# A two-layer mixture-of-experts block on one core: the loop for left-over tokens ahead of the experts' last half, and a final norm of one chain per token tile

## Chip, cores and metric

The kernel runs on one core of a Trainium2 chip. The metric is the device time of one execution in microseconds (us); smaller is better. Times shown are the median of three runs, with the lowest and the highest. The profile and its trace are of one execution.

## What is computed

The reference is a block of two post-norm layers over 256 latent tokens, with 256 context tokens that pass through the same weights (model width 1024, all in fp32). In each layer three token mixers (attention, gated linear attention, neighbourhood attention) are merged and normed, then a hierarchical mixture of 32 experts follows, and a last norm:

```python
def layer_norm(x, g, b):
    return layer_norm0(x) * g + b
...
    def expert_block(inp):
        xb, e = inp
        return (jax.nn.silu(xb @ w1[e]) * (xb @ w3[e])) @ w2[e]
```

`x = LayerNorm(alpha * x + gate2 * HierMoE(h2))`: each token chooses one group of experts and the two best experts in it; the outputs come back to the token weighted by its gates. The next layer begins with `h = LN0(x) * (1 + scale1) + shift1`. Layer 0 needs both streams (512 tokens, T = 4 tiles of 128), the experts of layer 1 only the latents (T = 2).

## The kernel before

Tokens stand on the partitions, a tile of [128, 1024] each (`x1[t]`). The 32 experts of a layer are worked on in halves of 128 slots: 14 halves in layer 0 (the experts ranked by load, with one, two or four experts in a half), 16 halves of two experts in layer 1. An expert has six pieces of weights of [128, 2048], 1 MB each: four of w1 and w3, two of w2. The tile buffers `ew`, `ewb` and a few spare ones hold 9 pieces in layer 0 and 14 in layer 1. SyncE (SP) issues every load, in the order of its queue, and each issue waits until the buffer's last reader is done.

`experts` (line 1471) goes through the halves. `front` gathers the tokens of two halves to XT. `body` makes the two first products: h <- ew, XT at line 1506, four parts for a half of two experts, one for each pair of pieces. `tail` calls `expert_tail` (line 1398): silu on ScalarE, act on VectorE, a transpose (aT, lines 1406 and 1407), then the second product Y <- ew, aT at line 1414 in two parts n = 0, 1 of 512 columns, each split into Yh (line 806, ScalarE) and Yl (line 807, VectorE). `combine` brings Y back to the tokens: cb (lines 1428 and 1429), ct = cb times gate (line 1431), x += ct (line 1432). The tail of half n stands behind the body of half n + 1, so that TensorE has the body to do while the small steps run; after the last body come the tails of the last two halves.

`overflow` (line 1533) takes the tokens that found no slot. Its `For_i` loop (line 1545) runs once for every block of 128 such tokens; the count is read from memory, and it is zero here in both layers. It stands behind `experts`. `final_norm` (line 1581) norms the tiles in batches of two with `stats_all` (lines 336 to 346: bn_stats for each tile, then Newton's method on columns of both tiles). In layer 0 ScalarE's identity (line 1596), VectorE's product with g (1597) and the sum with b (1598, on GpSimdE, POOL, but for one tile) follow, and two tiles are stored for later (line 1600); in layer 1 VectorE does it alone (lines 1589 and 1592) and the output is stored (1594). `final_loads` (line 1604) loads g and b, spread over the partitions (`lgb`, 2 x 512 KB). Then layer 1 begins: `modulation` loads wmod (line 493) for the products tmod (line 495), `norm_T` (line 532) norms again with `stats_all`, makes xh (line 539) on ScalarE and transposes it (hT, line 550); the projections pT of the mixers come next.

What the engines do in which order is set by a scheduler, which places every instruction by the priority of its place in the program and by its operands; `later(n)` puts pieces back. A program loop is a place that it doesn't schedule across: what stands ahead of the loop in an engine's order stays ahead of it.

Of the kernel before, what the change touches and what calls it, by code (L numbers as in the profile page):

```python
# [21 lines left out]
NL = 2  # L22
# [36 lines left out]
# columns of the per-partition biases  # L59
# [9 lines left out]
# sections of the constants  # L69
# [9 lines left out]
# ranks of the experts of layer 0, by load but for experts 0 and 1, whose weights come in early:  # L79
# with 128 slots, with 64, the others with 32; the order of their halves of 128 slots  # L80
# [29 lines left out]
def groups(l):  # L110
    """The experts (in layer 0 by rank of their load) that share 256 slots, in two halves of one, two or four experts"""
# [10 lines left out]
def _constants():  # L122
# [20 lines left out]
    # slots of the experts by rank  # L143
# [15 lines left out]
    # pairs of tokens of a block of 64 whose highest different bit is the level's  # L159
# [5 lines left out]
def _layout(inp):  # L165
    """The arrays of setup_inputs() as the program reads them."""
# [6 lines left out]
    # w_mod: [layer, group of four 512-column chunks, k tile, half of the group][partition][2 chunks x 512]  # L173
# [10 lines left out]
    # branches in the order in which they are merged: gla, attention, neighbourhood  # L184
# [42 lines left out]
    # the relative bias of every (query, key), outside of the window a constant; context keys have none  # L227
# [12 lines left out]
    # experts: [layer, expert][partition][six pieces of 2048]  # L240
# [9 lines left out]
class _Prog:  # L250
# [3 lines left out]
    # ---- tiles  # L254
# [14 lines left out]
    def rsqrt(self, v, w, tmp=None):  # L269
        """v ** -0.5 by Newton's method"""  # L270
# [34 lines left out]
    def norm0(self, x, xh, total=None):  # L305
        """xh = layer_norm0(x), both [128, 1024]; with the sums of x, ScalarE makes those of its squares"""
# [15 lines left out]
    def stats_all(self, xs, apart=False):  # L322
        """stats of tiles together: columns of means, of 1 / sqrt(var + eps), and of the opposites of their products"""
# [25 lines left out]
    def norm_quick(self, x, out, g, b):  # L349
        """out = layer_norm0(x) * g + b, on VectorE alone, and the sums of its rows; x is overwritten"""  # L350
# [7 lines left out]
    def norm(self, x, out, g, b, last=None):  # L358
        """layer_norm0(x) * g + b, in two steps"""
# [24 lines left out]
    def projT(self, l, n, ntok):  # L384
        """[128 columns of w_in, tokens] = w^T h^T"""
# [7 lines left out]
    def projM(self, l, names, kper, width, tiles, sub=None):  # L393
        """[tokens, columns of w_in] for the token tiles, one bank each"""
# [17 lines left out]
    # ---- constants  # L412
# [42 lines left out]
    def open(self, name, side, tags):  # L455
        """A pool that shares its place with the one that follows it on the same side"""
# [7 lines left out]
    def later(self, n=400):  # L464
        """What is traced here gives way to the next n instructions"""
# [4 lines left out]
    # ---- modulation  # L470
    def modulation(self, l, groups, tag="raw", tag2="b2", ps="mod"):
        """[128, 512] of group g: row 32 j + s holds 512-column chunk 4 g + j for the latents (s = 0) and the context (s = 1)"""
# [11 lines left out]
        for g in groups:  # L484
# [19 lines left out]
            # the columns: [partition, scale or shift, stream, k tile]  # L504
# [18 lines left out]
    def mod_row(self, l, q, s, tag="o4"):  # L523
        """A modulation vector on every partition: [128, 1024]"""
# [7 lines left out]
    def norm_T(self, l, xs):  # L532
        """h^T of the mixers: modulated layer_norm0 of the four token tiles, in two parts"""
        nc = self.nc
        xh = []
        for a in range(0, 4, NT[l]):
# [1174 lines left out]
```

## Time and profile before

| | |
|---|---|
| runs, median (lowest to highest) | 2171.39 us (2170.97 to 2172.95) |
| profiled execution, span | 2169.8 us |
| TensorE (PE) busy | 1989.3 us, 92% |
| VectorE (DVE) busy | 968.1 us, 45% |
| ScalarE (ACT) busy | 561.9 us, 26% |
| GpSimdE (POOL) busy | 272.2 us, 13% |
| loaded and stored | 562.41 MB, mean 259 GB/s |

The span runs from the first to the last instruction of the profiled execution; no other time is given for it, and the median of the runs is 1.6 us above it. In the rows, "x16" counts instructions, "[1.33 <-DMA ew]" is idle time of the engine ahead of them and what ended it, a name with "q" (SPq) is an engine's sequencer, where it waits or issues. PE entries are single passes: a product of the program has two of them where its operands are fp32. A share of busy time is a mean over stages with different limits, so the stages are read one by one.

### The profile page before, as it was taken

The page shows a single profiled execution, that of the slowest core. Times are in us where ns is not written, and L with a number is a line of the kernel's source. Part 1 is how long each engine was busy: PE and PEld are TensorE (multiplying, and loading weights), DVE is VectorE, ACT ScalarE, POOL GpSimd, SP SyncE. Part 2 cuts the span into 40 slices and gives each one's busy share as a digit, 9 for nine tenths or more (in the row PEclk, how much of TensorE's full clock was granted, in tenths as well). Part 3 has the DMA queues.
Part 4 walks back from the last instruction along what each step waited for, and adds up shares of the span by engine and source line. Part 5 has one row for each costly group of instructions (what it writes and reads, how often), then busy time and mean ns, then how long its engine had stood idle before and what let it go on. Part 6 is the DMA issues. An engine that isn't in the chain of part 4 may idle for free. (4 is left out here: it accounts for less than half of the span.)

```text
span 2169.8 us, 28061 instructions
## 1 busy us (share of the span) xinstructions
PE 1989.3 (92%) x10749; PEld 1179.2 (54%) x10749; DVE 968.1 (45%) x2236; ACT 561.9 (26%) x992; POOL 272.2 (13%) x260
## 2 busy tenths in 40 slices
PE   5999999999998898989899598999996999999995
PEld 2676766777885353445253165786795433333321
DVE  4676765564388131222022765766648222221213
ACT  3443334343333000000000254444543111010000
POOL 1322100011110010111011222100020000000000
PEclk9999999999999999999999798999997999999998
DMA  7436212223328899999998723632466999999995
GB/s 289 164 121 218 78 59 69 93 83 96 126 79 334 367 420 421 371 385 421 419 369 370 270 85 112 197 118 74 139 207 250 387 421 423 421 423 422 421 422 222
DMA packets 113987, 562.41 MB, mean 259 GB/s; under 512 B 13302, under 2 KB 14838, under 8 KB 72120
## 3 DMA queue, kind: packets, MB, share of 16 engines
q1 hardware_dynamic: 113272, 558.85, 66.9%
q8 instruction: 87, 1.43, 0.3%
q10 hardware_dynamic: 576, 1.70, 0.2%
q14 instruction: 52, 0.43, 0.1%
HBM read 557.36 MB, written 3.15 MB: 258 GB/s over the span
## 5 line engine op out<-in xcount | busy, mean ns | idle before, releaser
L1506 PE MATMUL h<-ew,XT 128*64 128x512 f32 (+2 forms) x2048 | 478.3, 611 | 40.0 <-DMA ew<-in_ew_dram 39.8
L1506 PEld LDWEIGHTS h<-ew,XT 128*64 128x64 f32 (+2 forms) x2048 | 146.6, 135 | 326.3 <-issue 248.8
L1414 PE MATMUL Y<-ew,aT 128*64 128x512 f32 (+2 forms) x1024 | 252.4, 598 | 10.1 <-DMA ew<-in_ew_dram 7.9
L292 DVE TENSOR_TENSOR wlo<-raw,whi 128x1024 fp32r<-128x1024 f32 (+1 forms) x140 | 178.9, 1278 | 139.6 <-ACT whi L291 138.4
L1432 POOL TENSOR_TENSOR x<-x,ct 128x512 f32<-128x512 f32 x82 | 105.0, 1307 | 1003.5 <-DVE ct L1431 879.8
L380 PE MATMUL pT<-hThi,whi 128*128 128x512 f32 (+1 forms) x576 | 202.9, 352 | 1.5 <-ACT whi L291 0.8
L291 ACT CAST whi<-raw 128x1024 fp32r<-128x1024 f32 (+1 forms) x140 | 145.4, 1039 | 226.5 <-PE pT L381 116.2
L382 PE MATMUL pT<-hThi,wlo 128*128 128x512 f32 (+1 forms) x576 | 202.3, 351 | 0.2 <-DVE wlo L292 0.2
L381 PE MATMUL pT<-hTlo,whi 128*128 128x512 f32 (+1 forms) x576 | 202.1, 351 | 0.0
L1403 DVE SCALAR_TENSOR_TENSOR act<-h,s,sl 128x512 f32<-128x512 f32 x30 | 22.5, 751 | 325.4 <-PE h L1506 270.5
L1414 PEld LDWEIGHTS Y<-ew,aT 128*64 128x64 f32 (+2 forms) x1024 | 76.0, 133 | 151.0 <-issue 125.7
L807 DVE TENSOR_TENSOR Yl<-Y,Yh 128x512 fp32r<-128x512 f32 x60 | 41.4, 690 | 257.2 <-ACT Yh L806 254.1
L806 ACT CAST Yh<-Y 128x512 fp32r<-128x512 f32 x60 | 35.2, 587 | 462.5 <-PE Y L1414 462.5
L380 PEld LDWEIGHTS pT<-hThi,whi 128*128 128x128 f32 x576 | 109.5, 190 | 22.4 <-issue 4.1
L382 PEld LDWEIGHTS pT<-hThi,wlo 128*128 128x128 f32 x576 | 109.5, 190 | 16.2 <-issue 2.9
L381 PEld LDWEIGHTS pT<-hTlo,whi 128*128 128x128 f32 x576 | 109.6, 190 | 15.2 <-issue 3.0
L380 PE MATMUL pM<-whi,hThi 128*128 128x512 f32 (+1 forms) x304 | 110.7, 370 | 3.6 <-ACT qTkT L645 1.9
L381 PE MATMUL pM<-wlo,hThi 128*128 128x512 f32 (+1 forms) x304 | 111.8, 369 | 0.0
L382 PE MATMUL pM<-whi,hTlo 128*128 128x512 f32 (+1 forms) x304 | 111.7, 368 | 0.0
L495 PE MATMUL mod<-wmod,sT 128*32 128x512 f32 x320 | 75.0, 624 | 23.4 <-DVE s L343 14.8
L1407 ACT COPY aT<-aT 128x512 f32<-128x512 f32 x30 | 17.6, 586 | 292.7 <-PE aT L1406 292.7
L1383 PE MATMUL XT<-OH,h2hi 128*128 128x256 f32 x352 | 89.1, 290 | 0.0
(363 smaller groups left out, 3093.4 us busy)
## 6 DMA issues: line engine op xcount, KB each, us to landing
ew<-in_ew_dram SPq DMA_DIRECT2D x326, 1024.0 KB, 13.8
raw<-in_w_dram SPq DMA_DIRECT2D x145, 512.0 KB, 3.7
ew<-in_ew_dram SPq DMA_DIRECT2D x116, 512.0 KB, 13.5
wmod<-in_wmod_dram SPq DMA_DIRECT2D x96, 512.0 KB, 6.1
nb<-in_nb_dram SPq DMA_DIRECT2D x32, 256.0 KB, 3.8
g<-md SPq DMA_DIRECT2D x12, 256.0 KB, 7.6
row<-in_ln_dram SPq DMA_DIRECT2D x4, 512.0 KB, 4.9
lgb<-in_ln_dram SPq DMA_DIRECT2D x4, 512.0 KB, 12.0
```

The lines of the kernel that those rows point to most:

```text
L291: self.nc.scalar.copy(hi, src)
L292: (eng or self.nc.vector).tensor_tensor(lo, src, hi.bitcast(F32), op=ALU.subtract)
L380: mm(out, lh, rh, start=start, stop=False)
L381: mm(out, lh, rl, start=False, stop=False)
L382: mm(out, ll, rh, start=False, stop=stop)
L495: nc.tensor.matmul(p[32 * j:32 * j + 32, :], self.sT[:, k, :], raws[j // 2][:, 512 * (j % 2):512 * (j % 2) + 512], start=k == 0, stop=k == 7)
L806: self.nc.scalar.copy(hi, src)
L807: self.nc.vector.tensor_tensor(lo, src, hi.bitcast(F32), op=ALU.subtract)
L1383: mm(p[:, w * j:w * j + w], self.h2s[t][part][:, 128 * k:128 * k + 128], OH[:, t], start=t == 0 and part == 0, stop=t == T - 1 and part == 1)
L1414: mm(y[m * i:m * i + m, :], aT[:, 128 * f + m * i:128 * f + m * i + m], w2(f, n, i), start=f == 0, stop=f == 3)
L1432: (nc.vector if last and n else nc.gpsimd).tensor_tensor(self.x1[t][:, ns], self.x1[t][:, ns], tmp, op=ALU.add)
L1506: mm(h[m * i:m * i + m, :], XTs[dp][:, k, 128 * pr + m * i:128 * pr + m * i + m], w[i, 2 * q + k // 4][k % 4], start=k == 0, stop=k == 7)
```

## The change

The edits, by function:

- `experts`: when the last half comes, four of its pieces are loaded, then the tail of the half before it is made, then `overflow`, then the last body. g and b are loaded ahead of the last tail, in both layers, to a tile of "e8".
- `load`: w2 of the last half comes in pieces of 512 KB, those of the two experts in turn; `expert_tail` loses the order by expert that it had there.
- `overflow`: the loop's body takes weights in pieces of [128, 512] in "ct" buffers, and gets the slots of its tokens by transposing the one-hot matrix.
- `final_norm`: for each tile one chain on VectorE: bn_stats, mean and variance, Newton's method on [128, 1], (x - mean) g, then r and b; in layer 0 the last step also sums the rows.
- `norm_T`, layer 1: from these sums ScalarE makes the sum of squares (Square), VectorE the root, ScalarE xh, tile by tile.
- `run`: `final_norm` comes before the buffers of layer 0 are given back and those of layer 1's mixers are opened.

```diff
     def norm_T(self, l, xs):
-        for a in range(0, 4, NT[l]):
+        for t in range(4 if l else 0):
+            h, st = self.t([128, 1024], ("whi", "wlo")[t % 2], name="xh"), self.small(20)
+            nmu, v, m = (st[:, i:i + 1] for i in range(3))
+            nc.vector.tensor_scalar(nmu, self.total[t], -1.0 / 1024, None, op0=ALU.mult)
+            nc.scalar.activation(h, xs[t], AF.Square, bias=nmu, accum_out=v)
+            nc.vector.tensor_scalar(v, v, 1.0 / 1024, EPS, op0=ALU.mult, op1=ALU.add)
+            r = self.rsqrt(v, 1, st[:, 3:6])
+            nc.vector.tensor_tensor(m, nmu, r, op=ALU.mult)
+            nc.scalar.activation(h, xs[t], AF.Identity, bias=m, scale=r)
+            xh.append(h)
+        for a in range(0, 0 if l else 4, NT[l]):
...
     def load(self, l, us, n, js, step=2048, most=99, after=None):
         for j in js:
+            if step < 2048:
+                xs = [self.t([128, 2048], "ew", name="ew") for _ in us]
+                self.nw += len(us)
+                for v in range(0, 2048, step):
+                    for i, x in enumerate(xs):
+                        self.nc.sync.dma_start(x[:, v:v + step], w["src"][i][:, j, v:v + step])
...
     def experts(self, l, T):
...
         def tail(dp, pr, us, hs):
-            end = SPL and 2 * dp + pr == len(halves) - 1
-            self.load(l, us, 2 * dp + pr, (4,))
-            self.load(l, us, 2 * dp + pr, (5,), 1024 if end else 2048)
+            end = 2 * dp + pr == len(halves) - 1
+            self.load(l, us, 2 * dp + pr, (4, 5), 1024 if end else 2048)
...
-            with self.later(0 if n else FIRST):
-                held[n] = body(*x)
-            if n:
+            if n == len(halves) - 1:
+                self.load(l, x[2], n, range(4), most=4)
+                tail(*halves[n - 1], held[n - 1])
+                self.overflow(l, T)
+            held[n] = body(*x)
+            if 0 < n < len(halves) - 1:
                 tail(*halves[n - 1], held[n - 1])
+        lgb = self.final_loads(l)
         tail(*halves[-1], held[len(halves) - 1])
+        return lgb
...
     def final_norm(self, l, T, lgb):
+        self.total = []
+        for t in range(T):
+            x, st = self.x1[t], self.small(20)
+            for i in range(2):
+                nc.vector.bn_stats(st[:, 6 * i:6 * i + 6], x[:, 512 * i:512 * i + 512])
+            nc.vector.bn_aggr(st[:, 12:14], st[:, 0:12])
+            mu, v = st[:, 12:13], st[:, 14:15]
+            nc.vector.tensor_scalar(v, st[:, 13:14], EPS, None, op0=ALU.add)
+            r = self.rsqrt(v, 1, st[:, 15:18])
+            STT(x, x, mu, g, op0=ALU.subtract, op1=ALU.mult)
+            if l == NL - 1:
+                for i in range(2):
+                    s = slice(512 * i, 512 * i + 512)
+                    STT(x[:, s], x[:, s], r, b[:, s], op0=ALU.mult, op1=ALU.add)
+                    nc.sync.dma_start(self.out[0, 128 * t:128 * t + 128, s], x[:, s])
+                continue
+            self.total.append(st[:, 18:19])
+            STT(x, x, r, b, op0=ALU.mult, op1=ALU.add, accum_out=st[:, 18:19])
+            if t < 2:
+                nc.sync.dma_start(self.x2[t], x)
...
     def run(self):
-            self.experts(l, T)
-            if l:
-                lgb = self.final_loads(l)
-            self.overflow(l, T)
+            lgb = self.experts(l, T)
+            xs = self.final_norm(l, T, lgb)
             if l == 0:
...
                 left, right = self.mixers(1)
-                lgb = self.final_loads(l)
-            xs = self.final_norm(l, T, lgb)
```

How the engines' orders change is seen at three places. In the rows an instruction's line is that of its own program (before: loop 1545, h 1506, Y 1414; changed: loop 1570, h 1524, Y 1423), and "waits" names the queues and engines that it waits for (DMAHW0 to 7 are queues of loads).

**TensorE at the end of layer 1.** In the changed program (Y_15927 is Y of half 14, h_16211 and h_16228 are the body of half 15, Y_16273 and Y_16284 its Y):

```order
L1423 MATMUL Y_15927<-ew_15899,aT_15905 64x512 [waits DMAHW6_49,PE_49]
L1423 MATMUL Y_15927<-ew_15901,aT_15905 64x512 [waits DMAHW7_49]
...
L1569 TENSOR_LOAD r_4_13744 [waits DVE_49]
L1570 COMPARE_AND_BRANCH
L1570 UNCONDITIONAL_BRANCH [waits PE_49]
...
L1524 MATMUL h_16211<-ew_13766,XT_15609 64x512
L1524 MATMUL h_16211<-ew_13768,XT_15609 64x512
...
L1524 MATMUL h_16228<-ew_16203,XT_15609 64x512
L1524 MATMUL h_16228<-ew_16205,XT_15609 64x512
...
L1423 MATMUL Y_16273<-ew_16248,aT_16262 64x512 [waits Activation_49]
...
L1423 MATMUL Y_16284<-ew_16254,aT_16262 64x512 [waits DMAHW2_49,PE_49]
```

Before (h_15836 is the body of half 15, Y_15874 and Y_15885 Y of half 14, Y_15921 Y of half 15), the body stood ahead of Y of half 14, and each piece's first product had its own wait for a load:

```order
L1406 MATMUL aT_15866<-cst,act_15862 128x128 x3
L1506 MATMUL h_15836<-ew_15813,XT_15525 64x512 [waits DMAHW5_49]
...
L1506 MATMUL h_15836<-ew_15815,XT_15525 64x512 [waits DMAHW6_49]
L1506 MATMUL h_15836<-ew_15817,XT_15525 64x512 [waits DMAHW7_49]
L1506 MATMUL h_15836<-ew_15815,XT_15525 64x512
...
L1414 MATMUL Y_15874<-ew_15853,aT_15863 64x512 [waits DMAHW0_49,Activation_49]
...
L1414 MATMUL Y_15885<-ew_15857,aT_15863 64x512 [waits DMAHW2_49,PE_49]
...
L1414 MATMUL Y_15921<-ew_13680,aT_15910 64x512 [waits DMAHW5_49]
```

The body of half 15 has moved behind the loop, where its products have no wait for a load; only the Y whose weights are loaded behind the loop has one.

**SyncE at the end of layer 1.** Before (ew_15811 to 15817 are w1 and w3 of half 15, ew_15853 to 15859 w2 of half 14, the pieces behind them w2 of half 15):

```order
L1463 DMA ew_15811<-in_ew_dram 128x2048 [waits DMAHW4_49,PE_49]
L1463 DMA ew_15813<-in_ew_dram 128x2048 [waits DMAHW5_49,PE_49]
...
L1463 DMA ew_15853<-in_ew_dram 128x2048 [waits DMAHW0_49,PE_49]
L1463 DMA ew_15855<-in_ew_dram 128x2048 [waits DMAHW1_49,PE_49]
L1463 DMA ew_15857<-in_ew_dram 128x2048 [waits DMAHW2_49,PE_49]
L1463 DMA ew_15859<-in_ew_dram 128x2048 [waits DMAHW3_49,PE_49]
L1468 DMA ew_13678<-in_ew_dram 128x1024 [waits DMAHW4_49,PE_49]
L1468 DMA ew_13680<-in_ew_dram 128x1024 [waits DMAHW5_49,PE_49]
...
L1468 DMA ew_13685<-in_ew_dram 128x1024 [waits DMAHW3_49,PE_49]
L1545 COMPARE_AND_BRANCH
```

In the changed program (ew_15895 to 15901 are w2 of half 14, ew_16203 to 16209 w1 and w3 of half 15, ew_16248, 16249, 16254 and 16255 its w2):

```order
L1481 DMA ew_15895<-in_ew_dram 128x2048 [waits DMAHW4_49,PE_49]
...
L1481 DMA ew_15901<-in_ew_dram 128x2048 [waits DMAHW7_49,PE_49]
L1481 DMA ew_16203<-in_ew_dram 128x2048 [waits DMAHW0_49,PE_49]
L1481 DMA ew_16205<-in_ew_dram 128x2048 [waits DMAHW1_49,PE_49]
L1481 DMA ew_16207<-in_ew_dram 128x2048 [waits DMAHW2_49,PE_49]
L1481 DMA ew_16209<-in_ew_dram 128x2048 [waits DMAHW3_49,PE_49]
L1464 DMA ew_16248<-in_ew_dram 128x1024 [waits DMAHW6_49,DMAHW4_49,PE_49]
L1464 DMA ew_16249<-in_ew_dram 128x1024 [waits DMAHW7_49,DMAHW5_49,PE_49]
...
L1570 COMPARE_AND_BRANCH
...
L1642 DMA lgb_16245<-in_ln_dram 128x1024 x2
L1464 DMA ew_16254<-in_ew_dram 128x1024 [waits PE_49]
L1464 DMA ew_16255<-in_ew_dram 128x1024 [waits PE_49]
```

w2 of half 14 is now loaded ahead of the last pieces of half 15's body; g and b and the second pair of w2 have moved behind the loop.

**SyncE between the layers.** Before (lgb are g and b of layer 0; wmod is for tmod of layer 1):

```order
L1463 DMA ew_8669<-in_ew_dram 128x1024 [waits DMAHW6_49]
L1545 COMPARE_AND_BRANCH
...
L1611 DMA lgb_9051<-in_ln_dram 128x1024
L1611 DMA lgb_9052<-in_ln_dram 128x1024
L493 DMA wmod_9238<-in_wmod_dram 128x1024
L493 DMA wmod_9239<-in_wmod_dram 128x1024
L493 DMA wmod_9246<-in_wmod_dram 128x1024 [waits DMAHW7_49]
```

In the changed program (ew_8946 to 8952 are pieces of the last half's body, cs is a table for the rope instructions on VectorE, x the stores):

```order
L1481 DMA ew_8946<-in_ew_dram 128x2048 [waits DMAHW5_49,PE_49]
...
L1481 DMA ew_8948<-in_ew_dram 128x2048 [waits DMAHW6_49,DMAHW2_49,PE_49]
...
L1481 DMA ew_8950<-in_ew_dram 128x2048 [waits DMAHW7_49,DMAHW3_49,PE_49]
L1570 COMPARE_AND_BRANCH
...
L1642 DMA lgb_8988<-in_ln_dram 128x1024 x2
...
L1481 DMA ew_8952<-in_ew_dram 128x2048 [waits PE_49]
...
L583 DMA cs_9408<-in_cst_dram 128x256 [waits DMAHW3_49,DMAHW7_49,DMAHW1_49,PE_49]
...
L1634 DMA x_0_77<-x_1063_5260 128x1024 [waits DMAHW5_49,DVE_49,Pool_49]
L1634 DMA x_1_78<-x_1077_5379 128x1024 [waits DMAHW6_49,DVE_49,Pool_49]
L493 DMA wmod_9322<-in_wmod_dram 128x1024 [waits DMAHW0_49]
L493 DMA wmod_9323<-in_wmod_dram 128x1024
```

Loads of the last half stand on both sides of the loop, and the loads of wmod have moved behind the stores of x, which wait for VectorE.

## Rows read from the trace of the kernel before

**Rows 1.** Stretches: us, busy of PE, PEld, DVE, ACT, POOL, clock, DMA share, GB/s.
```profile
700.00:1177.00 477.00, 440.26 (x2246) 200.81 (x2246) 105.79 (x185) 38.87 (x66) 61.08 (x48) 0.97 0.96 394
...
1187.00:1207.00 20.00, 15.22 (x53) 7.05 (x51) 10.01 (x16) 1.17 (x2) 5.02 (x4) 0.96 0.02 7
...
1680.00:2144.00 464.00, 444.56 (x2045) 174.70 (x2046) 97.60 (x178) 46.32 (x80) 36.38 (x28) 1.00 1.00 414
```

**Rows 2.** Waits of SyncE (SPq), 1170 to 1240: us, times, longest.
```profile
SPq L1545 <- remote: 26.6, 1, 26.6
```

**Rows 3.** Timeline of TensorE, end of layer 0: start, us, [idle before].
```profile
1144.07 3.65 PE L1506 MATMUL h<-ew,XT 128*64 128x512 f32 x14 [1.33 <-DMA ew<-in_ew_dram]
...
1156.56 3.65 PE L1506 MATMUL h<-ew,XT 128*64 128x512 f32 x16
...
1192.40 1.20 PE L1428 MATMUL cb<-Yh,C 128*128 128x512 f32 x4
...
1194.46 3.65 PE L1414 MATMUL Y<-ew,aT 128*64 128x512 f32 x8
...
1223.93 1.05 PE L495 MATMUL tmod<-wmod,sT 128*32 128x512 f32 x4 [0.23 <-DMA wmod<-in_wmod_dram]
...
1262.39 0.39 PE L380 MATMUL pT<-hThi,whi 128*128 128x256 f32 x1
```

**Rows 4.** Timeline of VectorE around the loop of layer 0.
```profile
1204.33 1.28 DVE L1432 TENSOR_TENSOR x<-x,ct 128x512 f32<-128x512 f32 x2
...
1206.24 0.69 DVE L1432 TENSOR_TENSOR x<-x,ct 128x512 f32<-128x512 f32 x1
1208.65 4.84 DVE L336 BATCH_NORM_STATS2 s<-x 128x6 f32<-128x512 f32 x8 [1.71 <-issue]
...
1214.89 0.29 DVE L343 SCALAR_TENSOR_TENSOR s<-s 128x2 f32<-128x2 f32 x2
```

**Rows 5.** Timeline of ScalarE behind it.
```profile
1207.82 1.86 ACTq L373 DMA_DIRECT2D raw<-in_w_dram  x3
...
1237.65 4.63 ACT L539 ACTIVATE xh<-x,s 128x1024 f32<-128x1024 f32 x4 [16.13 <-DVE s L346]
```

**Rows 6.** Groups between the layers, 1207 to 1262: count, busy us, mean ns, idle before.
```profile
L495 PE MATMUL tmod<-wmod,sT 128*32 128x512 f32 x64 | 20.0, 724 | 18.8 <-DMA wmod<-in_wmod_dram 18.8
...
L1597 DVE TENSOR_TENSOR x<-x,lgb 128x1024 f32<-128x1024 f32 x4 | 8.9, 2298 | 1.2 <-ACT x L1596 1.2
```

**Rows 7.** Timeline of TensorE, end of layer 1.
```profile
2114.26 3.65 PE L1506 MATMUL h<-ew,XT 128*64 128x512 f32 x16 [1.43 <-DMA ew<-in_ew_dram]
...
2119.25 3.65 PE L1506 MATMUL h<-ew,XT 128*64 128x512 f32 x16 [0.75 <-DMA ew<-in_ew_dram]
2124.20 3.22 PE L1506 MATMUL h<-ew,XT 128*64 128x512 f32 x13 [1.30 <-DMA ew<-in_ew_dram]
...
2146.68 3.66 PE L1414 MATMUL Y<-ew,aT 128*64 128x512 f32 x12
```

**Rows 8.** Stretches as in rows 1, around TensorE's pauses.
```profile
1206.00:1222.00 16.00, 4.32 (x10) 0.56 (x12) 12.89 (x43) 4.64 (x4) 2.55 (x1) 0.50 0.83 318
1222.00:1224.00 2.00, 1.77 (x10) 0.21 (x8) 2.00 (x2) 0.00 (x0) 2.00 (x2) 0.86 1.02 408
...
1234.00:1242.00 8.00, 3.04 (x12) 1.62 (x12) 5.25 (x43) 4.35 (x4) 0.00 (x0) 0.50 1.03 405
1242.00:1244.00 2.00, 2.00 (x12) 0.80 (x10) 0.91 (x3) 1.11 (x4) 0.00 (x0) 0.74 0.90 260
```

**Rows 9.** DMA issues of the page: count, KB, us from issue to landing.
```profile
raw<-in_w_dram SPq DMA_DIRECT2D x145, 512.0 KB, 3.7
```

**Rows 10.** Timeline of VectorE, end of layer 1.
```profile
2159.18 1.27 DVE L1589 SCALAR_TENSOR_TENSOR x<-x,s,lgb 128x1024 f32<-128x1024 f32 x1
...
2161.82 0.16 DVE L343 SCALAR_TENSOR_TENSOR s<-s 128x2 f32<-128x2 f32 x1
2162.02 0.16 DVE L344 TENSOR_TENSOR s<-s 128x2 f32<-128x2 f32 x1
```

More of the change, by code (lines that the diff above doesn't have):

```diff
@@ L1396, in spots, with expert_tail @@
         return C
-    def expert_tail(self, h1, h3, gate, w2, halves, end=False):
+    def expert_tail(self, h1, h3, gate, w2, halves):
         nc, mm = self.nc, self.nc.tensor.matmul
@@ L1411, in expert_tail @@
             m = 128 // halves
-            order = [(f, i) for f in range(4) for i in range(halves)]
-            for f, i in sorted(order, key=lambda x: x[1]) if end else order:
+            for f, i in [(f, i) for f in range(4) for i in range(halves)]:
                 mm(y[m * i:m * i + m, :], aT[:, 128 * f + m * i:128 * f + m * i + m], w2(f, n, i), start=f == 0, stop=f == 3)
@@ L1448, in load @@
         for j in js:
+            if step < 2048:
[4 more added lines that the diff above has]
+                        self.nc.sync.dma_start(x[:, v:v + step], w["src"][i][:, j, v:v + step])
+                for i, x in enumerate(xs):
+                    w[i, j] = [x[:, 512 * v:512 * v + 512] for v in range(4)]
+                continue
             for i in range(len(us)):
@@ L1461, in load @@
                         self.nc.gpsimd.tensor_copy(x[0:32, 0:1], after[0:32, 0:1])
-                    for v in range(0, 2048, step):
-                        self.nc.sync.dma_start(x[:, v:v + step], src[:, v:v + step])
+                    self.nc.sync.dma_start(x, src)
                     w[i, j] = [x[:, 512 * v:512 * v + 512] for v in range(4)]
@@ L1568, in overflow @@
                 for k in range(8):
-                    mm(h, XT[:, k], w[2 * m + k // 4][:, 512 * (k % 4):512 * (k % 4) + 512], start=k == 0, stop=k == 7)
+                    mm(h, XT[:, k], piece(8 * m + k), start=k == 0, stop=k == 7)
                 hs.append(h)
-            Y = self.expert_tail(hs[0], hs[1], gate, lambda f, n, i: w[4 + n][:, 512 * f:512 * f + 512], 1)
-            col = self.small(1)
-            nc.vector.tensor_tensor(col, sel, c["pcol"][:, 0:1], op=ALU.add)
-            self.combine([(self.spots(self.slot_rows(self.over, T), col, T),) + Y], T, False)
+            Y = self.expert_tail(hs[0], hs[1], gate, lambda f, n, i: piece(16 + 4 * n + f), 1)
+            p = self.ps("row")
+            for t in range(T):
+                nc.tensor.transpose(p[:, 128 * t:128 * t + 128], OH[:, t].bitcast(F32), self.ident)
+            C = self.t([128, 128 * T], "o1", F32R, "C")
+            nc.vector.tensor_copy(C, p[:, :128 * T])
+            self.combine([(C,) + Y], T, False)
             nc.vector.tensor_scalar(cnt, cnt, 1.0, None, op0=ALU.add)
@@ L1582, in final_norm @@
         nc = self.nc
-        x = self.x1
+        STT = nc.vector.scalar_tensor_tensor
         g, b = lgb
-        for a in range(0, T, NB[l]):
-            ts = range(a, a + NB[l])
-            for t, (mu, r, m) in zip(ts, self.stats_all([x[t] for t in ts], APF[l])):
-                if t in FQ[l]:
-                    nc.vector.scalar_tensor_tensor(x[t], x[t], mu, g, op0=ALU.subtract, op1=ALU.mult)
-                    for i in range(2):
-                        s = slice(512 * i, 512 * i + 512)
-                        nc.vector.scalar_tensor_tensor(x[t][:, s], x[t][:, s], r, b[:, s], op0=ALU.mult, op1=ALU.add)
-                        if l == NL - 1:
-                            nc.sync.dma_start(self.out[0, 128 * t:128 * t + 128, s], x[t][:, s])
-                else:
-                    nc.scalar.activation(x[t], x[t], AF.Identity, bias=m, scale=r)
-                    nc.vector.tensor_tensor(x[t], x[t], g, op=ALU.mult)
-                    (nc.vector if t in FD else nc.gpsimd).tensor_tensor(x[t], x[t], b, op=ALU.add)
-                if t < 2 and l < NL - 1:
-                    nc.sync.dma_start(self.x2[t], x[t])
@@ L1603, in final_loads @@
+        return self.x1
     def final_loads(self, l):
         nc = self.nc
-        if l:
-            x = self.t([128, 2, 1024], "e8", name="lgb")
-            lgb = [x[:, 0], x[:, 1]]
-        else:
-            lgb = [self.t([128, 1024], "g4", name="lgb") for _ in range(2)]
+        x = self.t([128, 2, 1024], "e8", name="lgb")
+        lgb = [x[:, 0], x[:, 1]]
         for i in range(2):
```

21 lines of the change are left out of this document (10 added, 11 removed).

## The prediction

> **What bounds the kernel now.** I read the busy time by stage first. In both expert stages the weights set the pace: the DMA engines are busy 0.96 of the time from 700 to 1177 us (layer 0) and 1.00 from 1680 to 2144 (layer 1); from 1187 to 1207 they stand at 0.02 [rows 1]. SyncE's waits say why: the engine that issues the loads sits 26.6 us at line 1545, the loop [rows 2]. The loop makes no trip (no instruction of its body is in the trace), but all engines meet there. Next the timelines. In layer 0 TensorE's last Y runs from 1194.46 to 1198.1 [rows 3]; VectorE adds until 1206.93, meets the others, and goes on 1.71 us later [rows 4]; from there a chain of two norms leads to the last xh of ScalarE, 1237.65 + 4.63 = 1242.28 [rows 5], on which layer 1's transposes hang. In layer 1 TensorE waits for each pair of 1 MB pieces: 2114.26, 2119.25, 2124.20 [rows 7], 4.98 us a pair, 2.49 a MB. The last Y ends at 2150.3, the span 19.5 us later.
>
> **The loop, layer 0.** The change puts the loop behind Y of half 12 and ahead of the last body, with weights in flight. In the order of the changed program the products behind the loop have no wait for the weights loaded ahead of it; those for weights loaded behind it do. So the loop itself must wait until every transfer in flight has landed. Everything here rests on this step.
> When does it release? At 1144.07 a piece has just landed [rows 3]. In the new order the tenth after it is the last that Y(12) needs: 1144.07 + 10 x 2.49 = 1169.0, and Y's second part takes 3.65: 1172.6. Only then is a slot free for the last MB ahead of the loop, ew_8950, which travels alone. 512 KB take 3.7 us from issue to landing in the mixers [rows 9], so 1 MB 3.7 + 1.25 = 4.95 (an estimate; bounds 2.49, as in a full stream, and 7.4, two times 3.7). I take 4.95, as nothing else is in flight: 1177.5. VectorE's 1.71 at the old loop [rows 4] holds the way in and out; half of it, 0.85, gives 1178.3.
> TensorE then runs the body, four parts of 3.65 [rows 3] = 14.6, with eight merges cb, 1.9 (four take 1.20 with the overlap at their ends [rows 3]). It has been idle for some 6 us, and the rows show what that does to its clock: granted 0.50 from 1206 to 1222 and from 1234 to 1242, and only 0.86 and 0.74 in the 2 us behind each [rows 8], with TensorE back at work after its waits in these stretches [rows 6]. I count 4.4 us at half, a loss of 2.2 (bounds 0 and 4.4). Body over at 1197.0; silu, act, transpose and copy 2.5 (each works on 128x512, for which the rows have 0.6 to 0.7 [rows 4]); two Y of 3.65 with 0.9 of merges between: 1207.7, against 1198.1. **+9.6 us.** The last weights, issued from 1178 on, land ahead of their use.
>
> **The norms between the layers.** From the last Y to the last xh it took 1242.28 - 1198.1 = 44.2. Now: cast and Yl, 0.65 each, to 1209.0. VectorE's queue has twelve rope instructions next, which wait for a table that SyncE loads only once Y has read its weights: 3.7 less the 0.9 that 384 KB fewer save, so 1210.4; twelve at 0.13 (between the two pitches below) give 1212.0. Then 6 ct and 4 adds at 0.64, 8 bn_stats at 0.605 [rows 4], 8 instructions of 128x1024 at 1.2 [rows 10] and 40 small ones at 0.10: 6.4 + 4.8 + 9.6 + 4.0 = 24.8, to 1236.8. What goes are ScalarE's identities, VectorE's multiplies (2.3 each, as GpSimdE worked beside them [rows 6]) and GpSimdE's adds. ScalarE then has its last Square 1.16, three DMA triggers 1.86 that stand in its queue, 1.9 for a cast and the small chain ahead of the identities, and the four of these, 4.63 [rows 5]: 1246.4. That is 38.7, **-5.5 us**, with the 1.7 at the loop in it.
> On the small instructions: where two chains alternate, a pair has a pitch of 0.20 [rows 4], so 0.10 each; one chain alone has 0.20 each [rows 10]. By that upper end the 40 cost 4 us more; four tiles give chains that alternate, so I take 0.10. [...]
> **Matmuls moved.** Each of the 16 wmod pieces feeds four tmod matmuls, 1.05 us together at full clock [rows 3]. Before, ten pieces' ran ahead of the transposes, where TensorE only waited, and six between them. In the new order two pieces' run ahead, eight between the transposes, six inside the projections pT behind. TensorE was busy 2.00 of 2 us between the transposes [rows 8], and the projections are dense, so all eight that lose their idle place count: 8 x 1.05 = **+8.4 us** (at least the six in the projections, 6.3).
> Moved loads: wmod's 16 x 512 KB stood right behind the loop; now SyncE issues them behind the x stores, which wait for the new norm, from about 1234. At 1.25 us each the tenth is there at 1247, four weights of the mixers at 1252, the rest at 1260. TensorE wants the first while it transposes, 1244 to 1256, and the last in the projections, which began at 1262.39 [rows 3] and now begin later. I cost that at nothing; the cover is thin, some 10 us if it goes.
> Layer 0 and boundary: 9.6 - 5.5 + 8.4 = +12.5.
>
> **The loop, layer 1.** The norm's 1 MB (lgb) now comes behind the loop, so the stream ahead is 2.5 us earlier. Counted from 2114.26 - 2.5 = 2111.8 in pairs of 4.98: half 14's two pairs of w2 land at 2116.7 and 2121.7, and Y(14) ends at 2125.4. Its slots take half 15's first pair of w2, which SyncE issues ahead of the loop, behind two pairs for half 15's body in the stream: 2126.7, 2131.7, 2136.7. Release about 2137.4. Before, TensorE did this body beside the transfers [rows 7]; now it is idle for 12 us and then has all of it to do: 2.2 for the clock, 14.6, four merges 1.2: 2155.4; silu to copy 2.5, Y 3.65 twice: 2165.2, against 2150.3. **+14.9 us.** The last pair, issued when the body frees slots at about 2149, lands by 2156 and doesn't bind. After Y: 19.5 before; now without the loop's 1.7, but with two chains of 128x1 for one of 128x2: 18.5. **-1.0.** Two edits cost nothing: w2 in interleaved halves (the pieces are there ahead of their use), and pieces of 512 columns in the loop's body (which doesn't run).
>
> Sum: 2169.8 + 12.5 + 13.9 = 2196.2 for the span. The runs' median, 2171.39, is 1.6 above the profiled span, so 2197.8; I say **2197.5**.
>
> **Rivals.**
> *The loop waits for the engines alone*, and weights in flight go on. Then layer 0 resumes at 1173.5 instead of 1178.3 with no loss of clock: 9.6 - 4.8 - 2.2 = 2.6, with the boundary +5.5. In layer 1 the body starts at 2126.3 and, held by its pairs alone, ends with its merges at 2142; Y's first part ends at 2148.5, the last at 2152.2: +1.9 - 1.0. Together +6.4: 2177.8. For it: the trace never shows the loop with a transfer in flight. Against it: the products behind it have no wait of their own. Chance 0.09.
> *Faster: the boundary hangs on the load queue, not on the norm.* TensorE's waits for wmod sum to 18.8 us there [rows 6], and SyncE is held 26.6 [rows 2]; with the loop early, SyncE is past it at 1178. If wmod came in from then on, under the last body and Y, its matmuls would run in TensorE's pauses, layer 0's 9.6 would lie under the loads, and the stretch would end 18.8 earlier: 13.9 - 18.8 = -4.9, 2166.5. It decides if wmod is issued before VectorE's last add. Against it: in the new order it stands behind the x stores. Chance 0.06.
> *Dearer than the sum*: the boundary's loads come late (+10), or the small instructions keep the pitch of one chain (+4) and the clock costs double (+2.2 in each layer): 2206 to 2212. Chance 0.12. The forecast keeps 0.73.
>
> **The numbers.** A measurement of this kernel can tell about 0.2% (4.3 us) from no change. The range 2177 to 2212 takes in the first rival and the dear case, with the bounds of loads and clock, and leaves out the fast one. Faster 0.06 is the second rival; same 0.06 is the first rival with a boundary that gains 2 us more than I think; slower 0.88.
>
> **What would show it.** Right: in layer 1 TensorE is idle some 12 us ahead of the loop, the DMA is nearly empty for a dozen us behind it, and the last Y ends 15 us later than before, plus what layer 0 and the boundary cost; in layer 0 the loop is over at about 1178, and the last xh comes 38 to 39 us behind the last Y; GpSimdE has no work in the norm. Wrong: body products right behind the loop while transfers still run, or waits for wmod of over 10 us behind the transposes.

## The result, and the profile after

The changed kernel takes **2195.79 us** (median of four runs, 2190.55 to 2197.33), the kernel before 2171.18 beside it: 1.0105 times as long, 95% interval 1.0085 to 1.0126. The forecast was 2197.5. The profiled execution took 2197.33 us, its span is 2195.6, 25.8 us longer than the span before.

TensorE's busy time on the page is within 0.5% of that before (1994.2 against 1989.3 us), while the span grew by 25.8. So most of the time went into waits.

```profile
span 2195.6 us, 28115 instructions
...
PE 1994.2 (91%) x10749; PEld 1180.2 (54%) x10749; DVE 963.9 (44%) x2269; ACT 562.3 (26%) x996; POOL 266.5 (12%) x257
```

The end of layer 0 on TensorE (timeline: start, us, instructions, [idle before]):

```profile
1150.24 7.13 PE L1423 MATMUL Y<-ew,aT 128*128 128x512 f32 x16
...
1171.55 3.65 PE L1423 MATMUL Y<-ew,aT 128*64 128x512 f32 x14 [1.32 <-DMA ew<-in_ew_dram]
...
1182.21 12.75 PE L1524 MATMUL h<-ew,XT 128*64 128x512 f32 x50 [7.02 <-DMA ew<-in_ew_dram]
...
1210.27 1.93 PE L1423 MATMUL Y<-ew,aT 128*64 128x512 f32 x6
```

Y of half 12 ends at 1175.20, TensorE stands for 7.02 us, and only then begins the last body; in [rows 3] that body ran from 1156.56 on. Where the 7 us come from stands in SyncE's queue, here its timeline between the last expert loads of layer 0 and the norms:

```profile
1150.34 24.38 SPq L1481 DMA_DIRECT2D ew<-in_ew_dram  x5
1182.04 0.82 SPq L1642 DMA_DIRECT2D lgb<-in_ln_dram  x2
...
1239.52 12.57 SPq L493 DMA_DIRECT2D wmod<-in_wmod_dram  x10
```

and its waits (us, times, longest), 1170 to 1190 and, below, 2136 to 2152:

```profile
SPq L1570 <- DMA ew<-in_ew_dram: 5.1, 1, 5.1
...
SPq L1570 <- DMA ew<-in_ew_dram: 9.1, 6, 2.5
```

Line 1570 is the loop. It makes no trip, but SyncE waits there until the transfers in flight have landed: 5.1 us for the one piece of layer 0, and six waits, 9.1 us together, in layer 1. In [rows 2] it waited 26.6 us at its loop, and no load is named there. The loads of wmod go out at 1239.52, behind the stores of x.

The end of layer 1 on TensorE, to be read against [rows 7]:

```profile
2126.83 1.94 PE L1423 MATMUL Y<-ew,aT 128*64 128x512 f32 x2 [5.58 <-DMA ew<-in_ew_dram]
...
2134.20 3.65 PE L1423 MATMUL Y<-ew,aT 128*64 128x512 f32 x14 [0.67 <-DMA ew<-in_ew_dram]
2149.71 13.70 PE L1524 MATMUL h<-ew,XT 128*64 128x512 f32 x50 [11.86 <-DMA ew<-in_ew_dram]
...
2170.35 7.09 PE L1423 MATMUL Y<-ew,aT 128*64 128x512 f32 x32 [0.68 <-ACT aT L1417]
```

Two pauses: 5.58 us ahead of Y of half 14, and 11.86 at the loop. The stretches around both loops (columns as in [rows 1]):

```profile
1180.00:1184.00 4.00, 1.78 (x6) 0.56 (x8) 0.06 (x1) 0.00 (x0) 0.00 (x0) 0.50 0.21 78
1184.00:1188.00 4.00, 4.00 (x20) 1.35 (x18) 0.00 (x0) 0.00 (x0) 0.00 (x0) 0.87 0.54 193
2142.00:2146.00 4.00, 0.00 (x0) 0.00 (x0) 0.00 (x0) 0.00 (x0) 0.00 (x0) 0.50 0.91 359
...
2150.00:2154.00 4.00, 4.00 (x10) 0.95 (x9) 0.00 (x0) 0.00 (x0) 0.00 (x0) 0.50 0.77 261
2154.00:2158.00 4.00, 4.00 (x20) 1.36 (x18) 0.00 (x0) 0.00 (x0) 0.00 (x0) 0.95 0.00 1
2158.00:2162.00 4.00, 4.00 (x22) 1.31 (x19) 0.00 (x0) 0.60 (x1) 0.00 (x0) 1.00 0.00 0
```

From 2142 to 2146 no engine computes while 0.91 of the DMA time is used: the drain. Behind it TensorE works at a granted clock of 0.50 for four us. From 2154 to 2162 the DMA is empty, as the last loads wait for slots that this body has to free; SyncE's wait for it is:

```profile
SPq L1464 <- PE h L1524: 12.4, 1, 12.4
```

The norms, first VectorE's chain (timeline):

```profile
1217.05 0.68 DVE L1440 TENSOR_TENSOR ct<-cb,g 128x512 f32<-128x512 f32 x1
...
1234.59 0.81 DVE L280 TENSOR_SCALAR s<-s 128x1 f32<-128x1 f32 x4
1235.32 0.36 DVE L281 SCALAR_TENSOR_TENSOR s<-s 128x1 f32<-128x1 f32 x4
...
1240.45 1.28 DVE L1632 SCALAR_TENSOR_TENSOR x<-x,s,lgb 128x1024 f32<-128x1024 f32 x1
```

and ScalarE's last xh:

```profile
1246.74 3.50 ACT L544 ACTIVATE xh<-x,s 128x1024 f32<-128x1024 f32 x3
```

The last xh ends at 1250.24, 38.04 us behind the last Y (44.17 before). Behind it the tmod products stand among the transposes and projections (TensorE), where [rows 3] had them earlier:

```profile
1244.16 3.22 PE L495 MATMUL tmod<-wmod,sT 128*32 128x512 f32 x8 [23.26 <-DVE s L280]
1247.31 1.97 PE L560 MATMUL hT<-cst,xh 128*128 128x128 f32 x8
...
1262.77 1.05 PE L495 MATMUL tmod<-wmod,sT 128*32 128x512 f32 x4
...
1271.47 0.58 PE L380 MATMUL pT<-hThi,whi 128*128 128x256 f32 x1
```

All profiled executions, cut at five marks of TensorE: A0 is the start of the 7.13 us of Y of half 11 in layer 0, Y0 the end of layer 0's last Y, pT the first projection of layer 1, A1 the first Y of half 13 in layer 1, Y1 the last Y. Each cell is the difference of two marks, in us; the runs e1 to e11 are those below (there is no e8).

| kernel | A0 | A0 to Y0 | Y0 to pT | pT to A1 | A1 to Y1 | Y1 to end |
|---|---|---|---|---|---|---|
| before | 1147.7 | 50.5 | 64.3 | 834.5 | 53.5 | 19.5 |
| after | 1150.2 | 62.0 | 59.3 | 837.9 | 68.0 | 18.2 |
| e1 loop back | 1148.9 | 49.8 | 56.7 | 835.9 | 53.3 | 19.4 |
| e2 loop layer 0 | 1148.4 | 61.8 | 58.0 | 836.6 | 53.3 | 19.3 |
| e3 loop layer 1 | 1150.1 | 49.8 | 57.7 | 839.1 | 67.3 | 18.1 |
| e4 no loop | 1150.2 | 51.4 | 58.3 | 846.9 | 59.8 | 18.6 |
| e5 old norms | 1152.9 | 61.2 | 64.2 | 835.7 | 68.5 | 18.2 |
| e6 norms alone | 1144.7 | 50.5 | 57.4 | 829.4 | 53.5 | 19.6 |
| e7 final norm alone | 1147.0 | 50.4 | 64.3 | 834.1 | 53.4 | 19.7 |
| e9 order alone | 1143.7 | 52.0 | 59.6 | 827.6 | 59.1 | 20.6 |
| e10 norm first | 1150.7 | 50.4 | 60.1 | 836.5 | 53.5 | 19.3 |
| e11 norms, no loop | 1146.3 | 50.4 | 58.2 | 836.4 | 54.2 | 16.5 |

A0 lies ahead of every edit, and up to it TensorE runs the same products in the same order in all twelve; it still moves between 1143.7 and 1152.9. So several us in the first column, and perhaps some in the long fourth, are not to be explained from an edit. The short columns repeat to within about one us where the program is the same there.

### The profile page after: what moved, and what is told of

Its sections match the earlier page's. It is cut to its first block, busy times and chain, and to the rows that moved or that the text cites. A ratio compares the mean times of both kernels' runs of the same rounds, so it can differ in the third digit from the quotient of the medians.

```text
span 2195.6 us, 28115 instructions
## 1 busy us (share of the span) xinstructions
PE 1994.2 (91%) x10749; PEld 1180.2 (54%) x10749; DVE 963.9 (44%) x2269; ACT 562.3 (26%) x996; POOL 266.5 (12%) x257
## 5 line engine op out<-in xcount | busy, mean ns | idle before, releaser
L1524 PE MATMUL h<-ew,XT 128*64 128x512 f32 (+2 forms) x2048 | 485.5, 624 | 57.3 <-DMA ew<-in_ew_dram 56.9
L1423 PE MATMUL Y<-ew,aT 128*64 128x512 f32 (+2 forms) x1024 | 249.0, 600 | 17.7 <-DMA ew<-in_ew_dram 14.1
```

The lines of the kernel that those rows point to most:

```text
L1423: mm(y[m * i:m * i + m, :], aT[:, 128 * f + m * i:128 * f + m * i + m], w2(f, n, i), start=f == 0, stop=f == 3)
L1524: mm(h[m * i:m * i + m, :], XTs[dp][:, k, 128 * pr + m * i:128 * pr + m * i + m], w[i, 2 * q + k // 4][k % 4], start=k == 0, stop=k == 7)
```

## The experiments

The theory: the loop waits for every transfer in flight, and this drain costs about 10 and 15 us; the norms gain some 5; the moved loads of wmod cost some 8. Rivals: the new order costs by itself, loop or not; the boundary hangs on the load queue.

**e1, the loop back behind the last tail, with the old order of the last half.** The rest of the change stays.

```diff
-            if n == len(halves) - 1:
-                self.load(l, x[2], n, range(4), most=4)
-                tail(*halves[n - 1], held[n - 1])
-                self.overflow(l, T)
             held[n] = body(*x)
-            if 0 < n < len(halves) - 1:
+            if n:
                 tail(*halves[n - 1], held[n - 1])
...
+        self.overflow(l, T)
```

> The changed kernel with the loop put back behind the last half's tail (and the tail of half n behind the body of half n + 1 to the end), everything else as changed. Theory (the loop drains the loads in flight and TensorE stands still meanwhile): what the two loops cost, some 11.5 us in layer 0 and 14.5 in layer 1, goes away; the loop's own 1.7 us comes back at two places and g and b of layer 0 (2.5 us of transfer) stand in the stream again. 2195.8 - 26 + 3.4 + 2.5 = about 2175, within 3 us. Rival (the loop's place is not the cause, the norm and the moved loads between the layers are): it stays above 2188.

Measured: 2167.10 us, ratio to the kernel before 0.9983 [0.9966, 0.9999]. So 28.7 us of the changed kernel are this one piece. That is more than was thought (2175, within 3, was expected), and the rest of the change is not dearer than before but, if anything, some 3 us better.

**e2 and e3, the loop and order ahead in one layer only.**

```diff
-            if n == len(halves) - 1:
+            if n == len(halves) - 1 and l == 0:
```

> The loop ahead of the last half in layer 0 alone; in layer 1 it stands behind the tails again. Theory: layer 1's 14.5 us go and 1.7 us of the loop at the end come back: about 2183. Rival (layer 0's place costs nothing, only layer 1's does): about 2172 to 2175, as without any loop ahead.

> The loop ahead of the last half in layer 1 alone. Theory: layer 0's 11.5 us go, 1.7 us of the loop and 2.5 us of transfer for g and b come back: about 2188. Rival (the costs of the two places are not additive, because the one hides behind the other): with the other run of one place, the two savings don't sum to that of the run with the loop back in both layers, by more than 4 us.

Measured: e2 2179.13, 1.0037 [1.0023, 1.0051]; e3 2181.23, 1.0049 [1.0032, 1.0066] (there `l == 1`). Against e1 that is +12.0 for layer 0 and +14.1 for layer 1, together 26.1 of 28.7: the layers add up. The medians lie 4 and 7 us under the expected ones, as e1's does by 8; the table has the loss where it belongs, in A0 to Y0 for e2 (61.8), in A1 to Y1 for e3 (67.3).

**e4, the changed kernel without the call of the loop**, to part the drain from the order.

```diff
-                self.overflow(l, T)
```

> The changed kernel without the loop for left-over tokens: that part of the computation is left out, no other line is changed, so the tail of the half before the last still stands ahead of the last body in the program. Theory (the price is the drain at the loop, not the new order of tail and body): with no drain the loads stream on and TensorE starts the last body as its weights come; about 2170 to 2174. Rival (the order itself costs, since Y of half n - 1 waits for its w2 before the last body may begin): TensorE still idles some 12 us ahead of the last body in layer 1 and the time stays above 2185.

Measured: 2186.69, 1.0066 [1.0046, 1.0086]: a miss by over 12 us, on the rival's side by the time. Two things are in it. In the fourth column it has 9 us more than the changed kernel, far from the edit: 4.7 up to the first h of layer 1, which stay open, and 4.2 behind it, where the weights stream at 417 GB/s instead of 421 or 422 (more at e11). In the fifth column layer 1 takes 59.8 where the old order takes 53.5 and the loop 68.0. TensorE in e4, end of layer 1:

```profile
2127.12 1.94 PE L1423 MATMUL Y<-ew,aT 128*64 128x512 f32 x2 [7.78 <-DMA ew<-in_ew_dram]
...
2135.18 5.32 PE L1524 MATMUL h<-ew,XT 128*64 128x512 f32 x24
...
2157.74 8.78 PE L1423 MATMUL Y<-ew,aT 128*64 128x512 f32 x32 [0.73 <-ACT aT L1417]
```

With no loop at all TensorE stands 7.78 us, not some 12 ahead of the last body as the rival said, but ahead of Y of half 14. Four pieces of half 15's body are loaded ahead of that Y's w2; they are there, but in TensorE's order the body comes behind that Y. In the old order the body ran as its pieces came ([rows 7]).

**e5, the changed kernel with the old `final_norm` and `norm_T`.**

```diff
-        for t in range(4 if l else 0):
...
-        for a in range(0, 0 if l else 4, NT[l]):
+        for a in range(0, 4, NT[l]):
```

> The changed kernel with the final norm and the norm ahead of layer 1 as they were before (batches of two tiles; ScalarE, VectorE and GpSimdE), the loop still ahead of the last half. Theory: the new norms shorten the way from the last Y to the last xh; without them some 4 to 7 us are added between the layers and about 1 at the end: 2200 to 2204. Rival (the shorter way came from the loop no longer standing in it, the new norms give nothing): 2194 to 2197.

Measured: 2202.42, 1.0137 [1.0110, 1.0164], as expected: the new norms save 6.6 us in the changed kernel by the medians, 4.9 of them in Y0 to pT. From the last Y to the last xh it took 43.3 (38.0 with the new ones).

**e6, the kernel before with the new `final_norm` and `norm_T` and nothing else.** The edit is e5's turned round.

> The kernel before with the new final norm and the new norm ahead of layer 1, and nothing else of the change: loop, loads and the place of the pools as before. Theory: VectorE's chain from 1208.65 is 4.8 for bn_stats, 9.6 for eight large instructions and some 4 for small ones, then Square, root and identities on ScalarE: the last xh at about 1236.5 instead of 1242.3, and a tail that is as long as before within 1 us: 2171.2 - 5.5 = about 2166. Rival (the stretch hangs on the loads of wmod, of which the last ahead of the transposes lands near 1232): no more than 2 us are gained, 2169 to 2171.

Measured: **2157.62** (ten runs, 2153.82 to 2166.28), 0.9951 [0.9935, 0.9966]: faster than both kernels, by 13 us and not the 5.5 expected. Y0 to pT gives 6.8 of it, as in e1 (7.6). 5.1 more lie between pT and A1, and in the profiles 3.0 ahead of A0, where no edit is. The stretch from the first projection to the first h of layer 1, in the kernel before (columns as in [rows 1]):

```profile
1262.39:1689.74 427.35, 394.48 (x2643) 320.67 (x2642) 283.02 (x686) 185.71 (x324) 57.37 (x78) 0.94 0.48 156
```

In e6:

```profile
1252.66:1673.56 420.90, 391.44 (x2643) 318.12 (x2642) 283.02 (x686) 185.30 (x324) 58.13 (x78) 0.95 0.46 158
```

The same instructions take TensorE 3.0 us less at a slightly higher clock, and its idle time is 3.4 less. The scheduler also put some of TensorE's products of the mixers in another order, though no edit is there; whether that is the cause was not tried. It isn't an accident of one execution: e9, with the same norms, takes 420.70 us for the same stretch.

**e7, only the new `final_norm`, with the old `norm_T`.**

> The kernel before with the new final norm alone; the norm ahead of layer 1 as before (its own bn_stats of four tiles, in batches of two). It tells how the gain splits. Expected: VectorE's 2.3 us products beside GpSimdE go, but the second round of bn_stats stays on its queue: about half of the gain of the run with both, 2168 to 2169. If the sums that the final norm hands on are worth nothing, as fast as the run with both.

Measured: 2168.93, 0.9993 [0.9981, 1.0004]: the expected time, but not for the expected reason. Where half of the gain was expected there is none: Y0 to pT is 64.3, as before. The chain per tile gains nothing while `norm_T` still reads all tiles a second time (timeline of VectorE; half of that round):

```profile
1228.31 2.47 DVE L336 BATCH_NORM_STATS2 s<-x 128x6 f32<-128x512 f32 x4
```

The gain comes when that second round goes. The new `norm_T` reads the sums of the new `final_norm`, so no run has it by itself.

**e9, e6 with the order of the last half alone**, the loop staying at the end.

```diff
-            with self.later(0 if n else FIRST):
-                held[n] = body(*x)
-            if n:
+            if n == len(halves) - 1:
+                self.load(l, x[2], n, range(4), most=4)
+                tail(*halves[n - 1], held[n - 1])
+            held[n] = body(*x)
+            if 0 < n < len(halves) - 1:
```

> The kernel with the new norms alone (2157.6 us), and in it only the order of the last half as the change has it: four pieces of the last half loaded, the tail of the half before it, then the last body. The loop stays behind everything, with no load in flight. The run without any loop was far from its expectation (2186.7, not 2170 to 2174), so the theory is now in two parts: in layer 1 most of the price is this order (the expert stage was 10.6 us longer than before without the loop, 14.6 with it), in layer 0 most is the drain (the last Y came 3.5 us later without the loop, 12 to 14 with it). Expected: 2157.6 + 10.6 + 3.5 = about 2172. Rival (the drain is nearly all, and the run without the loop was slow for another reason, such as the last w2 in late buffers): within 4 us of 2158.

Measured: 2168.75, 0.9995 [0.9980, 1.0011], 11 us over e6 by the medians, 7.5 by the spans. In the table it is +1.5 in layer 0 and +5.7 in layer 1, where 3.5 and 10.6 were expected; 4.4 of the 10.6, which came from e4, lay ahead of A1, in that run's slower stream. e4's pause is there again (TensorE, end of layer 1):

```profile
2103.10 1.94 PE L1424 MATMUL Y<-ew,aT 128*64 128x512 f32 x2 [7.74 <-DMA ew<-in_ew_dram]
```

**e10, e6 with the final norm moved ahead of layer 1's buffers**, as the change has it.

```diff
+                lgb = self.final_loads(l)
+            xs = self.final_norm(l, T, lgb)
...
-                lgb = self.final_loads(l)
-            xs = self.final_norm(l, T, lgb)
```

> The kernel with the new norms alone, and in it only the move of the final norm ahead of the place where layer 1's buffers are opened, with g and b loaded to a tile of the expert stage; loop and halves as before. Theory (the prediction's matmuls moved): SyncE issues the loads of wmod behind the x stores, so six pieces' tmod run inside the projections and two more between the transposes: 5 to 8 us more, 2163 to 2166. Rival (this move is free, and the run with the loop put back was slower than that with the norms alone because of the last w2 in halves): within 2 us of 2157.6.

Measured: 2170.92, 0.9988 [0.9975, 1.0002], 13 us over e6; 5 to 8 were expected. 6.0 of the difference stand in A0, ahead of the edit. Behind it, Y0 to pT has +2.6 and pT to A1 +7.1, together 9.8. SyncE's timeline shows the moved loads:

```profile
1228.35 1.53 SPq L1614 DMA_DIRECT2D x<-x  x2
1229.92 10.22 SPq L493 DMA_DIRECT2D wmod<-in_wmod_dram  x10
```

and TensorE's what they do:

```profile
1234.16 4.63 PE L495 MATMUL tmod<-wmod,sT 128*32 128x512 f32 x12 [28.90 <-DMA wmod<-in_wmod_dram]
```

wmod goes out behind the stores of x. TensorE's idle time ends only with it; most of the 28.90 us is the norm, in which it has nothing else to do. But 20 of the 64 tmod products now come behind the first pT, where e6 has none, and so fall into dense work. From the last xh to A1 it takes 856.2 us, e6 847.8.

**e11, e6 without the call of the loop**, for the load queue.

```diff
-            self.overflow(l, T)
```

> The kernel before with the new final norm and norm_T (the version that took 2157.6 us), and without the left-over loop, which makes no trip here: the part that takes left-over tokens is left out. It tells what the loop costs where it stood before. My theory: only the meeting of the engines goes, about 1.7 us in each layer, as no transfer is in flight there; wmod may load from the last weights on, but the chain of the norm still binds, so 2153 to 2155 us, and from the last Y of layer 0 to the last xh 36 to 38 us instead of 39.0. The rival (the boundary hangs on the load queue): wmod's matmuls move into TensorE's pauses and the waits for wmod go, some 15 us: 2142 us or less.

Measured: 2163.16, 0.9963 [0.9949, 0.9977]: not faster than e6 but 5.5 us slower, so the expected gain didn't come. On the question it was made for it is plain. SyncE's timeline:

```profile
1192.41 13.72 SPq L493 DMA_DIRECT2D wmod<-in_wmod_dram  x10
```

TensorE's:

```profile
1209.12 5.74 PE L495 MATMUL tmod<-wmod,sT 128*32 128x512 f32 x16 [6.13 <-DMA wmod<-in_wmod_dram]
1229.13 1.11 PE L560 MATMUL hT<-cst,xh 128*128 128x128 f32 x4 [14.27 <-ACT xh L544]
1230.17 1.92 PE L495 MATMUL tmod<-wmod,sT 128*32 128x512 f32 x4
...
1235.51 1.05 PE L495 MATMUL tmod<-wmod,sT 128*32 128x512 f32 x4
```

wmod is issued 13 us earlier than in e6, whose row is

```profile
1205.35 10.15 SPq L493 DMA_DIRECT2D wmod<-in_wmod_dram  x8
```

Half of its products run early, and TensorE then waits 14.27 us for xh. The last xh came 35.8 us behind the last Y (39.0 in e6), pT not earlier at all (58.2 and 57.4): TensorE comes back from that pause at a granted clock of 0.51 from 1229 to 1235 (e6: 0.72 from 1230 to 1236), and four products take 1.92 us there, 1.05 later. So the boundary doesn't hang on the load queue; TensorE waits for the norm. What ate the rest of the gain lies later: the mixers took 4.2 us more, and the weights of layer 1 streamed slower than in e6, whose row comes first (columns as in [rows 1]):

```profile
1720.00:2060.00 340.00, 328.56 (x1508) 128.21 (x1506) 72.25 (x117) 33.43 (x59) 31.21 (x24) 1.00 1.02 422
```

and e11's:

```profile
1720.00:2060.00 340.00, 326.05 (x1500) 127.53 (x1498) 71.26 (x116) 33.56 (x59) 31.36 (x24) 1.00 1.02 417
```

e4's:

```profile
1720.00:2060.00 340.00, 325.08 (x1504) 127.36 (x1500) 68.41 (x112) 34.03 (x60) 28.68 (x22) 1.00 1.02 417
```

422 and 417 GB/s: 340 us at the lower rate lose 4. The ten profiles of kernels that have the loop show 421 or 422 in this stretch, and the two without it, e4 and e11, 417. In layer 0, where the loop is still to come, those two stream like the others (400 and 401 GB/s in the 390 us up to 10 us ahead of A0, 399 to 404 elsewhere). So the lower rate goes with the loop's absence. How is open, but it means that a kernel without the loop is no clean measure of what the loop costs.

## Why the prediction was right, point by point

| term | predicted | measured |
|---|---|---|
| ahead of the edits (A0) | 0 | +2.6 |
| layer 0, loop and order | +9.6 | +11.5 |
| norms, last Y to last xh | -5.5 | -6.1 |
| wmod's products, last xh to A1 | +8.4 | +4.6 |
| layer 1, loop and order | +14.9 | +14.6 |
| behind the last Y | -1.0 | -1.3 |
| sum | +26.4 | +25.9 |

That the sum is right to half a us is luck: +2.6 from ahead of every edit and +1.9 in layer 0 stand against -3.8 at wmod's products and some smaller ones. The step at the loops, on which the most rested, was right: the loop waits for the transfers in flight.

**Layer 0.** Y of half 12 was forecast to end at 1172.6 and the body to begin at 1178.3; with the 2.6 us that came from ahead, 1175.2 and 1180.9. Measured: 1175.20 and 1182.21. Of the 7.02 us the lone piece holds 5.1, near the estimate of 4.95; the other 1.9 I put down to the meeting of the engines, for which I had taken half of 1.71. The body took 18.5 (forecast 18.7), the Ys 9.2 (8.2).

**Norms.** VectorE's chain from 1217.05 to 1241.73 is 24.7; forecast 24.8. On the small instructions both pitches read from the rows came again: four at line 281 take 0.36 us, 0.09 each, four at line 280 take 0.81, 0.20 each. A single one of line 281 lasts 0.15 us here (from 1232.39), but the next begins before it ends (at 1232.46).

**wmod's products.** That they cost time where they now stand held; how much, the runs don't settle. In the changed kernel the first z of the mixers behind pT comes 35.4 us behind it instead of 25.2, so the products do push dense work back by more than the forecast 8.4; in e10, where only the final norm is moved, it is 31.7. From the last xh to A1, e10 takes 8.4 us more than e6, which has the same norms: the forecast's figure. Against the kernel before it is +4.6 in the changed kernel, and +1.9 in e5, with the old norms and as many products behind pT. The stretch in the changed kernel, against the two shown with e6:

```profile
1271.47:1702.15 430.68, 400.91 (x2671) 321.73 (x2670) 282.09 (x687) 185.72 (x324) 59.03 (x78) 0.95 0.48 156
```

TensorE is busy 6.4 us longer than before (394.48), the stretch only 3.3. There are two readings. Idle time in the mixers may have taken half of the load, which I had costed as if they had none. Or the changed kernel also has what e6 gains here, 6.8 us from the last xh to A1 (854.6 before, 847.8 in e6), which no term foresaw, and this hides part of the products' price. No run tells the two apart, so the 4.6 is not shown to be the size of this term alone. In e1, which has the same move, pT to A1 is only 1.4 us longer than before.

**Layer 1.** The times are those forecast, moved by the 12.5 us that stand ahead: Y of half 14 ends at 2137.85 (2125.4 + 12.5), the body begins at 2149.71 (2137.4 + 12.5), the last Y ends at 2177.44 (2165.2 + 12.5). **What was off is the split.** The prediction put the 14.9 on the loop's wait, and its first rival priced this order without a drain at +1.9, which leaves 13.0 for the drain. By e4 and e9 the order alone costs about 6 us (59.8 and 59.1 against 53.5), and the changed kernel with its drain takes 8 to 9 more (68.0). The rival's 1.9 has the load of g and b out of the way, for which the prediction takes 2.5 us; in e4 and e9 SyncE still issues it some 17 us ahead of A1, in the stream, as before. Without it some 3.5 us are left for the order and some 11 for the drain (estimates: 6 - 2.5, and 14.6 less that), so the order was priced too low and the drain too high. In layer 0 the split is 1 to 1.5 for the order and 10 for the drain, against 2.6 and 7.0 in the prediction. The prediction saw that TensorE would no longer run the body beside the transfers, but put this down to the loop; the order of TensorE and of the loads, with two pairs of the next body ahead of w2 of half 14, does it too.

**Rivals.** That the loop waits for the engines alone is out: SyncE's waits at line 1570 name the loads. That the boundary hangs on the load queue is out by e11, where wmod comes 13 us earlier and pT does not. The clock cost about what was taken: 50 products of the body at 0.228 us (3.65 / 16) would be 11.4, and took 12.75 and 13.70; 1.3 and 2.3 lost, against 2.2 each. The cover for wmod's transfers held: in the changed kernel TensorE has no wait for wmod between 1205 and 1290. As forecast, GpSimdE does nothing from 1221 to 1252, in the norm. The DMA was empty behind the loop of layer 1 for 8 us, not for a dozen, as g and b fill the first four (0.77 from 2150 to 2154).

What stays open: the up to 9 us by which A0 differs between runs, how the loop's absence slows the stream of layer 1, the 4.7 and 4.2 us that the mixers of e4 and e11 take more, and what e6 and e9 gain there.

## What to carry to other kernels

In this program a loop that makes no trip was still a point where the engines met and where SyncE waited for the transfers in flight (5.1 us for loads in layer 0, 9.1 in layer 1). In a program built like it, put such a loop where the load queue is empty anyway, and keep it out of a stretch that streams weights. When one edit both moves such a meeting point and changes an order, price each by itself; a right sum can hide a split that is off. Taking the loop out is not a clean way to price it: both kernels without it had a slower stream far behind its place (417 GB/s against 421 or 422). And the gain at the norm came with taking the second reading of the rows off VectorE (sums as a by-product, squares on ScalarE: Y0 to pT 57.4 in e6), not with the new chains of the final norm alone (64.3 in e7, as before). The new norms without the rest were the best version here (2157.62 us).

## What was not expected of the hardware

The same stream of layer 1's weights ran at 421 or 422 GB/s in the ten kernels with the loop and at 417 in the two without it, with the DMA engines at the same busy share (1.02); the loop of layer 0 makes no trip and stands over 450 us ahead. From the first h of layer 1 to A1 this is 411.4 and 411.5 us against 406.9 to 408.5, as large as some of the edits under study. And A0, which lies ahead of every edit, spread over 9 us between the profiled executions.
